# A mixture-of-experts encoder: the overflow part as a small loop ahead of expert 0, and the last tile's norms around the routing

## The chip, the cores and the metric

The kernel runs on one core of a Trainium2 chip. The metric is the device time of one execution in microseconds (us), the median of several runs. The engines have short names: PE is TensorE, which multiplies matrices, with PEld for its weight loads; DVE is VectorE, ACT is ScalarE, POOL is GpSimd, SP is SyncE, which here does little but issue DMA transfers. Each engine works through its own queue of instructions in order and waits on semaphores for the others.

## The reference

Two layers, 512 tokens of 1024 columns. Each layer has a token mixer (two kinds of attention with gates) and a mixture of 16 experts, of which each token uses two; the group of experts and the two inside it are chosen from sigmoid scores. Cut to what the change touches:

```
def _layer_norm(x, g=None, b=None):
    mu = jnp.mean(xf, -1, keepdims=True)
    var = jnp.mean(jnp.square(xf - mu), -1, keepdims=True)
    y = (xf - mu) * lax.rsqrt(var + LN_EPS)
...
def _rms_norm(x, g):
    y = xf * lax.rsqrt(jnp.mean(jnp.square(xf), -1, keepdims=True) + RMS_EPS)
    return (y * g.astype(jnp.float32)).astype(x.dtype)
...
    qa = _apply_rope(_rms_norm(qa.reshape(b, s, A_HEADS, HEAD_DIM), qn_g), cos, sin)
    ka = _apply_rope(_rms_norm(ka.reshape(b, s, A_KV_HEADS, HEAD_DIM), kn_g), cos, sin)
...
def _moe(h, w_router, router_bias, w_gate, w_up, w_down):
    scores = jax.nn.sigmoid((t @ w_router).astype(jnp.float32))
    sel = scores + router_bias.astype(jnp.float32)
    grp_score = jnp.sum(lax.top_k(sel.reshape(-1, N_GROUPS, EXPERTS_PER_GROUP), TOP_K)[0], -1)
    best = jnp.argmax(grp_score, axis=-1)
    ...
    _, idx = lax.top_k(jnp.where(in_group, sel, -jnp.inf), TOP_K)
    ...
    act = jax.nn.silu(hg) * hu * combine[..., None].astype(t.dtype)
    y = jnp.einsum('tef,efd->td', act, w_down)
...
    for l in range(DEPTH):
        ...
        h = _layer_norm(x) * (1.0 + sc1) + sh1
        mix = _mixer(h, w_in[l], q_norm_g[l], k_norm_g[l], w_branch_a[l], w_branch_b[l],
                     w_out[l], cos, sin, slopes)
        x = _layer_norm(DN_ALPHA * x + g1 * mix, ln1_g[l], ln1_b[l])
        h = _layer_norm(x) * (1.0 + sc2) + sh2
        ffn = _moe(h, w_router, router_bias, w_gate, w_up, w_down)
        x = _layer_norm(DN_ALPHA * x + g2 * ffn, ln2_g[l], ln2_b[l])
```

## The kernel before

The 512 tokens are four tiles of 128 (t = 0 to 3). Products are in a split form: an operand is cast to a rounded part (`wH`, `xH`, on ACT) and the rest is subtracted (`wL`, `xL`, on DVE), and PE makes three products of the parts. A scheduler orders the instructions of a stretch of straight code on each engine; a run-time condition (`tc.If`) cuts the program, and nothing is moved across it.

A layer runs through its stages in this order: norm and first modulation, the input projection, rope and attention, the gates, the output projection with the residual, the routing, the experts, and the combine with the last norm.

*Norms.* `stats` makes mean and variance on DVE (`mv`), and `pool_rsqrt` takes the reciprocal root on POOL in two steps, a multiply-add (L285) and a power (L286). `norm` applies it: the first columns by two passes of DVE (L321, L323), the rest, from CUT or CUTH on, by ACT (L319) and two steps of POOL (L325, L326). The rope (`rope(t)`) uses `pool_rsqrt` for the norms of ten heads, the name `rs`: DVE makes the sums of squares `ss`, goes on with products that don't need `rs`, and needs it at L604; `q` follows at L608, and PE transposes it at L620.

*Last tile and routing.* `tile_x1(t)` makes the normed residual x1 and `tile_h2(t)` the second norm h2, which SP stores to `h2d` in memory (L971). After the last tile ACT takes the sigmoid of the scores (L996). DVE and PE make ranks and positions; `vt` (L1066) is the list of tokens of each expert. POOL gathers the rows of h2d for an expert through that list (`xe`, L1104), so the gather needs `vt` and all four stores.

*Experts.* Each expert has room for CAP = 128 tokens. The loop over 16 experts has x_load (the gather, two experts ahead), x_split, x_gate, x_up and x_down; the weights are streamed by SP, 1 MB for each of gate, up and down, with up to ten loads asked for ahead of the routing. `cnti` is the count of the fullest expert. `overflow()` treats what lies over CAP: each engine loads `cnti` (L1204) and branches on it (L1206). It is called in the loop at e == EIF = 5, with NPRE = 4 weight loads issued ahead of it. With these inputs the body isn't entered.

Of the kernel before, what the change touches and what calls it, by code (L numbers as in the profile page):

```python
# [8 lines left out]
F32 = mybir.dt.float32  # L9
# [9 lines left out]
P = 128  # L19
S = 512  # L20
# [67 lines left out]
def build(tc, A, out):  # L88
    nc = tc.nc
    with ExitStack() as es:  # L90
# [192 lines left out]
        def pool_rsqrt(name, src, eps, mult, n):  # L283
            r = small(name, [n])
            PO.tensor_scalar(r, src, mult, eps, op0=OP.mult, op1=OP.add)  # L285
            PO.tensor_tensor(r, r, mhalf[:, :n], op=OP.pow)  # L286
            return r
# [12 lines left out]
        def stats(src):  # L300
# [5 lines left out]
            r = pool_rsqrt("rstd", mv[:, 1:2], LN_EPS, 1.0, 1)  # L306
# [6 lines left out]
        def norm(src, name, g, b, st=None, cut=None):  # L313
# [4 lines left out]
            for p, z in parts(src, cut, D):  # L318
                issued["act"] = ACT.activation(n[:, z], p, AF.Identity, bias=nb, scale=r)  # L319
# [110 lines left out]
        def layer(l, hH, hL, W0, after=None, qk=None):  # L430
# [17 lines left out]
            with ExitStack() as order:  # L448
              if after is not None:
                order.enter_context(tc.issue_after(after.ins))  # L450
              V.tensor_scalar(gq[:, 0, :], gq[:, 0, :], 0.125, None, op0=OP.mult)
# [136 lines left out]
            def rope(t):  # L588
# [5 lines left out]
                rs = pool_rsqrt("rs", ss, RMS_EPS, 1.0 / HD, 10)  # L594
# [344 lines left out]
            x1, r1 = [], []  # L939
# [10 lines left out]
            def tile_x1(t):  # L950
# [9 lines left out]
                n = norm(xr[t], "x1", r_g, r_b, st)  # L960
# [4 lines left out]
            def tile_h2(t):  # L965
# [4 lines left out]
                n2 = norm(n, "h2", r_sc2, r_sh2, st, CUTH)  # L970
                SY.dma_start(h2d[tcols(t), :], n2)  # L971
                if t < NT - 1:
                    ACT.mul(n, n, ALPHA)
# [23 lines left out]
            with tc.issue_after(sig.ins):  # L997
                ACT.mul(x1[NT - 1], x1[NT - 1], ALPHA)
# [17 lines left out]
            two = g4(sel).rearrange("p n (a b) -> p n a b", b=2)  # L1016
            mx, mn = rt("mx", [NTG, 2]), rt("mn", [NTG, 2])
            V.tensor_tensor(mx, two[:, :, :, 0], two[:, :, :, 1], op=OP.max)
            V.tensor_tensor(mn, two[:, :, :, 0], two[:, :, :, 1], op=OP.min)
            gs, gs2 = rt("gs", [NT, NG]), rt("gs2", [NT, NG])  # L1020
            fl = lambda z: z.rearrange("p t g -> p (t g)")
            V.tensor_tensor(fl(gs2), mx[:, :, 0], mx[:, :, 1], op=OP.min)
            V.tensor_tensor(mn[:, :, 0], mn[:, :, 0], mn[:, :, 1], op=OP.max)
            V.tensor_tensor(fl(gs), mx[:, :, 0], mx[:, :, 1], op=OP.max)
            V.tensor_tensor(fl(gs2), fl(gs2), mn[:, :, 0], op=OP.max)
            V.tensor_add(gs, gs, gs2)
# [31 lines left out]
            for k in range(2):  # L1058
                for t in range(NT):
                    at = ats[:, NT * k + t]  # L1060
                    V.tensor_scalar(at, iotab, sv[:, 0, k, t:t + 1], None, op0=OP.is_equal)
                    for i in range(2):
                        PE.matmul(mp, lhsT=at, rhs=src[:, NT * k + t, 2 * i:2 * i + 2], start=(k == 0 and t == 0 and i == 0),
                                  stop=(k == 1 and t == NT - 1 and i == 1))
            vt = small("vt", [2, NE], I32, bufs=1)
# [16 lines left out]
            V.tensor_mul(gm, gm, gt)  # L1082
            go = rt("go", [2, NT])
            V.tensor_sub(go, gt, gm)
            cnt = rt("cnt", [1])
            V.reduce_max(cnt, posf[:, NT, :], axis=X)
            cnti = small("cnti", [1], I32, bufs=1)
            V.tensor_copy(cnti, cnt)

# [97 lines left out]
            def keep_weights():  # L1187

                for i in range(NKEEP):
                    e = NE - NKEEP + i  # L1190
                    we = rt("we", [2, NT])
                    V.tensor_mul(we, o12[:, :, :, e], gm)
                    V.tensor_sub(gm, gm, we)
# [8 lines left out]
            def overflow():  # L1202
# [3 lines left out]
                with tc.If(rv > CAP):  # L1206
                    ovf = sco
                    V.tensor_mul(tmp, o12, go[:, :, :, None].to_broadcast([P, 2, NT, NE]))
                    V.tensor_add(ovf, tmp[:, 0], tmp[:, 1])
                    with tc.For_i(0, NE, 1) as e:  # L1210
                        def blocks(w, tags, view):
                            r = []
                            for i, tag in enumerate(tags):
                                z = wp.tile([P, 512], F32, tag=tag, name="f" + w, bufs=NWH)
                                SY.dma_start(*view(z, A["w_exp_" + w][l][bass.ds(e, 1)], i))
# [8 lines left out]
                        for k in range(2):  # L1224
                            SY.dma_start(fd[k], A["w_exp_down"][l][bass.ds(e, 1)][0, P * k:P * k + P])
                        for t in range(NT):
                            xe = rp.tile([P, D], F32, tag="row", name="fx")
                            SY.dma_start(xe, h2d[tcols(t), :])
                            xT = rp.tile([P, 8, P], F32, tag="row", name="fxT")
# [176 lines left out]
```

## Time and profile before

| | us |
|---|---|
| time before, median of 3 runs (lowest, highest) | 1416.98 (1414.26, 1420.20) |
| profiled execution | 1411.59 |
| its span | 1409.6 |
| PE busy | 1283.9 |
| DVE busy | 1018.3 |
| ACT busy | 717.1 |
| POOL busy | 292.8 |

The span runs from the first to the last instruction that the profiler records; the rest of the execution's time lies around it. Busy times overlap, since the engines run beside each other. The granted clock of PE over the span is 0.954 of full speed. A row of a timeline gives the start, the duration, the engine and the line, then what was written and read; the bracket gives how long the engine was idle before it and which instruction of which engine, or which transfer, released it.

### The profile page before, as it was taken

The page shows a single profiled execution, that of the slowest core. Times are in us where ns is not written, and L with a number is a line of the kernel's source. Part 1 is how long each engine was busy: PE and PEld are TensorE (multiplying, and loading weights), DVE is VectorE, ACT ScalarE, POOL GpSimd, SP SyncE. Part 2 cuts the span into 40 slices and gives each one's busy share as a digit, 9 for nine tenths or more (in the row PEclk, how much of TensorE's full clock was granted, in tenths as well). Part 3 has the DMA queues.
Part 4 walks back from the last instruction along what each step waited for, and adds up shares of the span by engine and source line. Part 5 has one row for each costly group of instructions (what it writes and reads, how often), then busy time and mean ns, then how long its engine had stood idle before and what let it go on. Part 6 is the DMA issues. An engine that isn't in the chain of part 4 may idle for free. (4 is left out here: it accounts for less than half of the span.)

```text
span 1409.6 us, 21666 instructions
## 1 busy us (share of the span) xinstructions
PE 1283.9 (91%) x7953; PEld 1043.7 (74%) x7953; DVE 1018.3 (72%) x1944; ACT 717.1 (51%) x1504; POOL 292.8 (21%) x317
## 2 busy tenths in 40 slices
PE   4898999999998949899889899999999894989986
PEld 4787777677778848788659787767777794878862
DVE  5877877776367779899787876563336767879985
ACT  2344444555744337677554444455564532767760
POOL 1142000000013652222352200000000266122224
PEclk9799999999999969999999999999999996999998
DMA  9646555466066197899644454122215527779952
GB/s 319 213 151 248 197 179 172 150 190 192 30 195 209 60 299 255 275 346 333 240 144 150 150 179 150 61 75 76 75 51 173 196 75 255 263 255 347 355 207 79
DMA packets 182992, 266.77 MB, mean 189 GB/s; under 512 B 18665, under 2 KB 131721, under 8 KB 182880
## 3 DMA queue, kind: packets, MB, share of 16 engines
q1 hardware_dynamic: 159312, 225.46, 48.2%
q0 software_dynamic: 11456, 24.07, 4.9%
q10 hardware_dynamic: 12112, 15.78, 3.7%
q8 instruction: 66, 1.08, 0.3%
q14 instruction: 46, 0.38, 0.1%
HBM read 250.79 MB, written 27.30 MB: 197 GB/s over the span
## 5 line engine op out<-in xcount | busy, mean ns | idle before, releaser
L216 DVE TENSOR_TENSOR wL<-raw,wH 128x512 fp32r<-128x512 f32 x520 | 350.8, 703 | 75.6 <-ACT wH L215 64.3
L215 ACT CAST wH<-raw 128x512 fp32r<-128x512 f32 x520 | 318.3, 622 | 160.2 <-PE mm L1173 41.6
L225 PE MATMUL mm<-hH,wH 128*128 128x512 f32 x512 | 206.9, 404 | 0.0
L226 PE MATMUL mm<-hL,wH 128*128 128x512 f32 x512 | 202.9, 396 | 0.0
L227 PE MATMUL mm<-hH,wL 128*128 128x512 f32 x512 | 202.5, 395 | 0.0
L225 PE MATMUL mm<-wH,xH 128*128 128x256 f32 x512 | 150.5, 294 | 2.0 <-ACT xH L343 1.2
L227 PE MATMUL mm<-wH,xL 128*128 128x256 f32 x512 | 149.4, 292 | 0.7 <-DVE xL L344 0.7
L226 PE MATMUL mm<-wL,xH 128*128 128x256 f32 x512 | 147.4, 288 | 0.7 <-DVE wL L216 0.7
L249 DVE SCALAR_TENSOR_TENSOR acc<-araw,cond,acc 128x512 f32<-128x512 f32 x148 | 110.8, 749 | 5.4 <-DMA araw<-in_w_ada 2.2
L227 PEld LDWEIGHTS mm<-hH,wL 128*128 128x128 f32 x512 | 96.4, 188 | 21.0 <-issue 1.1
L225 PEld LDWEIGHTS mm<-hH,wH 128*128 128x128 f32 x512 | 96.7, 189 | 20.2 <-issue 1.2
L226 PEld LDWEIGHTS mm<-hL,wH 128*128 128x128 f32 x512 | 96.6, 189 | 19.2 <-issue 0.3
L225 PEld LDWEIGHTS mm<-wH,xH 128*128 128x128 f32 x512 | 100.5, 196 | 4.3 <-ACT xH L343 2.1
L226 PEld LDWEIGHTS mm<-wL,xH 128*128 128x128 f32 x512 | 100.0, 195 | 2.6 <-DVE wL L216 1.4
L227 PEld LDWEIGHTS mm<-wH,xL 128*128 128x128 f32 x512 | 99.7, 195 | 1.6 <-DVE xL L344 1.1
L225 PE MATMUL mm<-wH,hH 128*128 128x256 f32 (+1 forms) x272 | 81.5, 300 | 4.8 <-ACT hH L412 3.1
L227 PE MATMUL mm<-wH,hL 128*128 128x256 f32 (+1 forms) x272 | 80.8, 299 | 2.0 <-DVE hL L378 0.7
L226 PE MATMUL mm<-wL,hH 128*128 128x256 f32 (+1 forms) x272 | 80.3, 296 | 0.1
L1178 POOL DMA_INDIRECT y<-ye,vt x28 | 33.5, 1198 | 221.8 <-DVE ye L1174 221.8
L281 POOL DMA_DIRECT2D mod<-adar x8 | 4.2, 531 | 331.1 <-ACT adar L280 331.1
L1173 PE MATMUL mm<-raw,eT 128*128 128x512 f32 x128 | 65.9, 639 | 5.1 <-ACT eT L1156 3.1
L745 DVE TENSOR_TENSOR zB<-sB,biasB 128x256 f32<-128x256 f32 (+2 forms) x48 | 22.9, 488 | 59.9 <-PE sB L743 26.1
(319 smaller groups left out, 2873.9 us busy)
## 6 DMA issues: line engine op xcount, KB each, us to landing
araw<-in_w_ada SPq DMA_DIRECT2D x44, 1024.0 KB, 5.3
raw<-in_w_in SPq DMA_DIRECT2D x40, 1024.0 KB, 5.2
raw<-in_w_exp_gate SPq DMA_DIRECT2D x32, 1024.0 KB, 8.7
raw<-in_w_exp_up SPq DMA_DIRECT2D x28, 1024.0 KB, 9.7
raw<-in_w_exp_down SPq DMA_DIRECT2D x28, 1024.0 KB, 7.5
raw<-in_w_out SPq DMA_DIRECT2D x8, 1024.0 KB, 5.2
y<-y SPq DMA_DIRECT2D x16, 512.0 KB, 8.0
eraw<-in_w_ada SPq DMA_DIRECT2D x4, 1024.0 KB, 14.6
```

The lines of the kernel that those rows point to most:

```text
L215: ACT.copy(H, raw(s))
L216: V.tensor_sub(L, raw(s), H.bitcast(F32))
L225: PE.matmul(o, lhsT=lH, rhs=rH, start=(i == 0), stop=False)
L226: PE.matmul(o, lhsT=lH, rhs=rL, start=False, stop=False)
L227: PE.matmul(o, lhsT=lL, rhs=rH, start=False, stop=(i == n - 1))
L249: last = V.scalar_tensor_tensor(acc, raw[:, k, :], ck, acc, op0=OP.mult, op1=OP.add)
L281: PO.dma_start(moddr[l, kind].rearrange("o (k n) -> (o k) n", n=P), r[0:8, :])
L745: V.tensor_add(z, s[:, :, 0:wid], biasB[g][:, ii::2, j0:j0 + wid])
L1173: PE.matmul(p, lhsT=a, rhs=w, start=(i == 0), stop=(i == len(todo) - 1))
L1178: st = PO.indirect_dma_start(out=y2, out_offset=bass.IndirectOffsetOnAxis(ap=vidx[:, e:e + 1], axis=0), in_=ye, in_offset=None, bounds_che ...
```

## The change

The overflow part is called once ahead of `x_split(0)` and no longer in the loop. Its body loops over the tiles instead of being written out four times, issues its loads on ACT's queue, and stores its rows to `y2` in memory by an indirect DMA, where the combine reads all rows, instead of adding into x1; so the combine uses `gt` for all tokens. `cnti` is reduced straight from the positions. In `pool_rsqrt` the sum with eps is made on DVE and only the power stays on POOL; the factor 1/64 of the head norm goes into eps and the gains. For the last tile, x1 is normed on DVE over all columns; of h2 only the first pass is made ahead of the routing, the second is made of two ACT products and two POOL sums behind the sigmoid, and the store follows them. The group score is the largest of six pair sums instead of two minima and maxima.

```
-        def pool_rsqrt(name, src, eps, mult, n):
+        def pool_rsqrt(name, src, eps, n):
             r = small(name, [n])
-            PO.tensor_scalar(r, src, mult, eps, op0=OP.mult, op1=OP.add)
+            V.tensor_scalar(r, src, eps, None, op0=OP.add)
             PO.tensor_tensor(r, r, mhalf[:, :n], op=OP.pow)
...
-            r = pool_rsqrt("rstd", mv[:, 1:2], LN_EPS, 1.0, 1)
+            r = pool_rsqrt("rstd", mv[:, 1:2], LN_EPS, 1)
...
-            for p, z in parts(src, cut, D):
+            for p, z in parts(src, cut, D) if cut < D else []:
...
-              V.tensor_scalar(gq[:, 0, :], gq[:, 0, :], 0.125, None, op0=OP.mult)
+              V.tensor_scalar(gq[:, 1, :], gq[:, 1, :], 8.0, None, op0=OP.mult)
...
-                rs = pool_rsqrt("rs", ss, RMS_EPS, 1.0 / HD, 10)
+                rs = pool_rsqrt("rs", ss, RMS_EPS * HD, 10)
...
-                n = norm(xr[t], "x1", r_g, r_b, st)
+                n = norm(xr[t], "x1", r_g, r_b, st, D if t == NT - 1 else None)
...
-                n2 = norm(n, "h2", r_sc2, r_sh2, st, CUTH)
+                if t < NT - 1:
+                    n2 = norm(n, "h2", r_sc2, r_sh2, st, CUTH)
+                    ACT.mul(n, n, ALPHA)
+                else:
+                    n2 = f4("h2", [D])
+                    V.scalar_tensor_tensor(n2, n, st[0], r_sc2, op0=OP.subtract, op1=OP.mult)
+                    LAST.append((n2, st[1]))
+                    return
                 SY.dma_start(h2d[tcols(t), :], n2)
-                if t < NT - 1:
-                    ACT.mul(n, n, ALPHA)
...
             sig = ACT.activation(sco, sco, AF.Sigmoid)
             with tc.issue_after(sig.ins):
+                n2, r = LAST[0]
+                for i in range(2):
+                    z = slice(512 * i, 512 * i + 512)
+                    ACT.mul(n2[:, z], n2[:, z], r)
+                    PO.tensor_tensor(n2[:, z], n2[:, z], r_sh2[:, z], op=OP.add)
+                SY.dma_start(h2d[tcols(NT - 1), :], n2)
                 ACT.mul(x1[NT - 1], x1[NT - 1], ALPHA)
...
-            two = g4(sel).rearrange("p n (a b) -> p n a b", b=2)
-            mx, mn = rt("mx", [NTG, 2]), rt("mn", [NTG, 2])
-            V.tensor_tensor(mx, two[:, :, :, 0], two[:, :, :, 1], op=OP.max)
-            V.tensor_tensor(mn, two[:, :, :, 0], two[:, :, :, 1], op=OP.min)
-            gs, gs2 = rt("gs", [NT, NG]), rt("gs2", [NT, NG])
             fl = lambda z: z.rearrange("p t g -> p (t g)")
-            V.tensor_tensor(fl(gs2), mx[:, :, 0], mx[:, :, 1], op=OP.min)
-            V.tensor_tensor(mn[:, :, 0], mn[:, :, 0], mn[:, :, 1], op=OP.max)
-            V.tensor_tensor(fl(gs), mx[:, :, 0], mx[:, :, 1], op=OP.max)
-            V.tensor_tensor(fl(gs2), fl(gs2), mn[:, :, 0], op=OP.max)
-            V.tensor_add(gs, gs, gs2)
+            duo = rt("duo", [NTG, 6])
+            v4s, at = g4(sel), 0
+            for d in range(1, 4):
+                V.tensor_add(duo[:, :, at:at + 4 - d], v4s[:, :, 0:4 - d], v4s[:, :, d:4])
+                at += 4 - d
+            gs = rt("gs", [NT, NG])
+            V.tensor_reduce(fl(gs), duo, axis=X, op=OP.max)
...
+            cnti = small("cnti", [1], I32, bufs=1)
+            V.tensor_reduce(cnti, pos[:, NT, :], axis=X, op=OP.max)
...
-            V.tensor_mul(gm, gm, gt)
-            go = rt("go", [2, NT])
-            V.tensor_sub(go, gt, gm)
-            cnt = rt("cnt", [1])
-            V.reduce_max(cnt, posf[:, NT, :], axis=X)
-            cnti = small("cnti", [1], I32, bufs=1)
-            V.tensor_copy(cnti, cnt)
...
-                    V.tensor_mul(we, o12[:, :, :, e], gm)
-                    V.tensor_sub(gm, gm, we)
+                    V.tensor_mul(we, o12[:, :, :, e], gt)
+                    V.tensor_mul(we, we, gm)
+                    V.tensor_sub(gt, gt, we)
...
                 with tc.If(rv > CAP):
-                    ovf = sco
-                    V.tensor_mul(tmp, o12, go[:, :, :, None].to_broadcast([P, 2, NT, NE]))
-                    V.tensor_add(ovf, tmp[:, 0], tmp[:, 1])
+                    row = rt("row", [2, NT])
+                    V.tensor_scalar(row, sv[:, 0], float(CAP), None, op0=OP.is_ge)
+                    code = rt("code", [2, NT])
+                    encs = enc.rearrange("p (k t) (i j) -> p k t i j", k=2, i=2)
+                    V.tensor_add(code, encs[:, :, :, 0, 0], encs[:, :, :, 1, 0])
+                    V.tensor_mul(row, row, code)
+                    oc = sc("oc", [2, NT, NE])
+                    V.tensor_mul(oc, o12, row[:, :, :, None].to_broadcast([P, 2, NT, NE]))
+                    V.tensor_add(oc[:, 0], oc[:, 0], oc[:, 1])
+                    oi = sc("oi", [NE * NT], I32)
+                    V.tensor_scalar(oi.rearrange("p (e t) -> p t e", t=NT), oc[:, 0], -1.0, float(2 * S), op0=OP.mult, op1=OP.add)
+                    sh = sc("sh", [NE * NT], I32)
                     with tc.For_i(0, NE, 1) as e:
...
-                        for t in range(NT):
-                            xe = rp.tile([P, D], F32, tag="row", name="fx")
-                            SY.dma_start(xe, h2d[tcols(t), :])
-                            xT = rp.tile([P, 8, P], F32, tag="row", name="fxT")
+                            ACT.dma_start(fd[k], A["w_exp_down"][l][bass.ds(e, 1)][0, P * k:P * k + P])
+                        with tc.For_i(0, S, P) as t:
+                            xe = f4("fx", [D])
+                            ACT.dma_start(xe, h2d[bass.ds(t, P), :])
...
+                            PO.indirect_dma_start(
+                                out=y2, out_offset=bass.IndirectOffsetOnAxis(ap=oi[:, 0:1], axis=0),
+                                in_=fy, in_offset=None, bounds_check=2 * S - 1, oob_is_err=False)
...
+            overflow()
             x_split(0)
...
-                if e == EIF:
-                    for ew in [ew for ew in order3[3 * e:] if ew not in PRE][:NPRE]:
-                        PRE[ew] = wraw(x_src(*ew), x_shape(ew[1]), tags[ew])
-                    overflow()
```

On SP, at the end of the loads ahead of the routing in layer 0, before (`h2d` is the second norm in memory, h_4934 that of the last tile, the `raw` names are expert weights):

```order
L192 DMA raw_4963<-in_w_exp_gate 128x8x256
L971 DMA h2d_4265<-h_4934 128x1024
L189 DMA raw_4949<-in_w_exp_up 128x4x256
L189 DMA raw_4950<-in_w_exp_up 128x4x256
L189 DMA raw_4953<-in_w_exp_down 128x1024
L189 DMA raw_4954<-in_w_exp_down 128x1024
L192 DMA raw<-in_w_exp_down 128x2x1024
L192 DMA raw<-in_w_exp_gate 128x8x256
L192 DMA raw<-in_w_exp_up 128x8x256
```

and of the changed kernel:

```order
L192 DMA raw_4955<-in_w_exp_gate 128x8x256
L189 DMA raw_4941<-in_w_exp_up 128x4x256
L189 DMA raw_4942<-in_w_exp_up 128x4x256
L189 DMA raw_4945<-in_w_exp_down 128x1024
L189 DMA raw_4946<-in_w_exp_down 128x1024
L1008 DMA h2d_4265<-h_4931 128x1024
L1207 TENSOR_LOAD cnti
L1209 COMPARE_AND_BRANCH
```

The store of the last tile has moved behind the four loads of the L189 helper, and the branch follows the store.

On PE in layer 0, around the load of the count and its branch, before (`tp` is a transpose, of the token rows `xe` and of the hidden rows `ea` of an expert; `mm` are the products):

```order
L336 MATMUL tp<-c_ident,xe 128x128 x4
L1204 TENSOR_LOAD cnti
L1206 COMPARE_AND_BRANCH
...
L1206 UNCONDITIONAL_BRANCH
L336 MATMUL tp<-c_ident,ea 128x128 x2
L336 MATMUL tp<-c_ident,xe 128x128 x4
L225 MATMUL mm<-wH,xH 128x256
L226 MATMUL mm<-wL,xH 128x256
```

and of the changed kernel:

```order
L1071 MATMUL mp<-src,ats 128x32
L1207 TENSOR_LOAD cnti
L1209 COMPARE_AND_BRANCH
...
L1209 UNCONDITIONAL_BRANCH
L336 MATMUL tp<-c_ident,xe 128x128 x8
L225 MATMUL mm<-wH,xH 128x256
L226 MATMUL mm<-wL,xH 128x256
L227 MATMUL mm<-wH,xL 128x256
```

The branch stood between two transposes of `xe`, and now stands between the last routing product `mp` and the first transpose of `xe` for expert 0.

On DVE in layer 0, from the normalized gates `gt` on, before:

```order
L1079 TENSOR_TENSOR rt_gt<-rt_sv,rt_den 128x8
L216 TENSOR_TENSOR wL<-raw,wH 128x512
L1082 TENSOR_TENSOR rt_gm<-rt_gm,rt_gt 128x8
L216 TENSOR_TENSOR wL<-raw,wH 128x512
L1084 TENSOR_TENSOR rt_go<-rt_gt,rt_gm 128x8
L216 TENSOR_TENSOR wL<-raw,wH 128x512
L1192 TENSOR_TENSOR rt_we<-rt_o_5001,rt_gm 128x8
L1193 TENSOR_TENSOR rt_gm<-rt_gm,rt_we 128x8
L1194 TENSOR_TENSOR rt_we<-rt_we 128x4
L344 TENSOR_TENSOR xL<-tp,xH 128x512 x2
L216 TENSOR_TENSOR wL<-raw,wH 128x512 x4
L1136 TENSOR_TENSOR ea<-ea,mm 128x256
```

and of the changed kernel:

```order
L1196 TENSOR_TENSOR rt_gt<-rt_gt,rt_we 128x8
L1197 TENSOR_TENSOR rt_we<-rt_we 128x4
L1207 TENSOR_LOAD cnti
L1209 COMPARE_AND_BRANCH
L1211 TENSOR_SCALAR rt_row<-rt_sv 128x8
...
L1209 UNCONDITIONAL_BRANCH
L216 TENSOR_TENSOR wL<-raw,wH 128x512 x3
L344 TENSOR_TENSOR xL<-tp,xH 128x512
L216 TENSOR_TENSOR wL<-raw,wH 128x512
L344 TENSOR_TENSOR xL<-tp,xH 128x512
L216 TENSOR_TENSOR wL<-raw,wH 128x512 x6
```

The subtractions `wL` that stood between the small routing steps now stand behind the branch, three of them ahead of the first `xL`.

## Rows read from the trace of the kernel before

**Rows 1.** The page, part 1: engine, busy us (share of the span), instructions.

```profile
PE 1283.9 (91%) x7953; PEld 1043.7 (74%) x7953; DVE 1018.3 (72%) x1944; ACT 717.1 (51%) x1504; POOL 292.8 (21%) x317
```

**Rows 2.** Times by stretch: us; busy per engine (count); clock, DMA share, GB/s.

```profile
560.38:570.62 10.24, 10.16 (x69) 8.69 (x68) 8.41 (x15) 6.04 (x12) 2.52 (x2) 1.00 0.97 315
570.62:585.93 15.31, 11.82 (x71) 10.20 (x70) 11.10 (x18) 9.76 (x19) 2.22 (x2) 0.89 0.62 203
585.93:596.30 10.37, 10.29 (x70) 8.81 (x69) 9.54 (x18) 8.01 (x16) 2.52 (x2) 1.00 1.02 339
...
1246.91:1263.66 16.75, 12.50 (x71) 10.45 (x70) 11.09 (x18) 9.76 (x19) 2.22 (x2) 0.90 0.55 176
```

**Rows 3.** Lines L1206, L1204 (ns min/median/max) and the matmul behind, from the timeline.

```profile
L1206 PEldq COMPARE_BRANCH  x2: 3836/3968/4101, 569.4 to 1245.5; - x2
...
L1206 DVEq COMPARE_BRANCH  x2: 56/64/72, 572.6 to 1248.6; - x2
...
L1204 PEldq TENSOR_LOAD <-cnti x2: 314/402/490, 568.8 to 1245.1; - x2
...
573.78 0.66 PE L336 MATMUL tp<-c_ident,ea 128*128 128x128 f32 x2 [2.75 <-PEq L1206]
```

**Rows 4.** Timeline ahead of expert 0: start us, us, work [idle <-releaser].

```profile
515.78 1.94 PE L336 MATMUL tp<-c_ident,xe 128*128 128x128 f32 x8 [5.87 <-DMA xe<-h2d,vt]
...
1192.41 1.94 PE L336 MATMUL tp<-c_ident,xe 128*128 128x128 f32 x8 [5.95 <-DMA xe<-h2d,vt]
...
510.98 1.44 POOL L1104 DMA_INDIRECT xe<-h2d,vt  x1 [4.19 <-DVE rt_cnt L1086]
```

**Rows 5.** Timeline of DVE in expert 0.

```profile
520.18 0.69 DVE L216 TENSOR_TENSOR wL<-raw,wH 128x512 fp32r<-128x512 f32 x1 [1.11 <-ACT wH L215]
```

**Rows 6.** Timeline from the last tile's norm to the list of tokens.

```profile
499.33 0.69 DVE L303 BATCH_NORM_STATS2 st<-x 128x6 f32<-128x512 f32 x1 [1.66 <-POOL x L326]
...
502.37 0.49 ACT L319 ACTIVATE h<-x,nb,rstd 128x128 f32<-128x128 f32 x1 [4.68 <-POOL nb L308]
...
509.95 0.19 DVE L1066 TENSOR_TENSOR vt<-c_none,mp 128x32 int32<-128x32 f32 x1 [0.25 <-PE mp L1063]
```

**Rows 7.** Timeline of SP's issues: start us, us to issue.

```profile
493.84 0.49 SPq L192 DMA_DIRECT2D raw<-in_w_exp_gate  x1
504.15 0.34 SPq L971 DMA_DIRECT2D h2d<-h  x1
```

**Rows 8.** DMA issued at 493.84, 504.15, 555.49, 556.01, 1169.58: KB, us to landing.

```profile
raw<-in_w_exp_gate SPq DMA_DIRECT2D x1, 1024.0 KB, 10.3
...
h2d<-h SPq DMA_DIRECT2D x1, 512.0 KB, 3.1
...
raw<-in_w_exp_gate SPq DMA_DIRECT2D x1, 1024.0 KB, 7.4
...
raw<-in_w_exp_up SPq DMA_DIRECT2D x1, 1024.0 KB, 12.6
...
raw<-in_w_exp_gate SPq DMA_DIRECT2D x1, 1024.0 KB, 9.8
```

**Rows 9.** Lines L285, L286; PE's waits in 75:130 and 720:806 (us, times, longest).

```profile
L285 POOL TENSOR_SCALAR rs<-ss x8: 308/3020/3658, 80.3 to 791.1; 128x10 f32<-128x10 f32 x8
...
L286 POOL TENSOR_TENSOR rs<-rs,c_mhalf x8: 1954/1962/3074, 81.8 to 792.6; 128x10 f32<-128x10 f32 x8
...
PE tp L620 <- DVE q L608: 4.0, 3, 2.2
...
PE tp L620 <- DVE q L608: 4.9, 2, 2.7
```

**Rows 10.** Timeline of POOL in the tail.

```profile
1397.75 0.18 POOL L285 TENSOR_SCALAR rstd<-mv 128x1 f32<-128x1 f32 x1 [0.96 <-DVE mv L305]
```

**Rows 11.** DMA issued at 581.04 and 643.18: KB, us to landing.

```profile
raw<-in_w_exp_gate SPq DMA_DIRECT2D x1, 1024.0 KB, 5.7
...
raw<-in_w_exp_gate SPq DMA_DIRECT2D x1, 1024.0 KB, 12.7
```

## What the change was predicted to do

> **What bounds the kernel now.** I read the page first: TensorE (PE) is busy for 91% of the span [rows 1]. So a microsecond is to be had only where PE stands still or runs at a lower granted clock, and for each edit I asked what ended PE's idle time there. Next came the table of engine times by stretch of the expert loop: an expert takes 10.2 to 10.4 us with PE busy for all but 0.1 of it, but the stretch in which expert 5 begins, where the skip of the overflow part stands, takes 15.31 us in layer 0 and 16.75 in layer 1, with PE busy for 11.82 and 12.50 and a mean clock of 0.89 and 0.90 instead of 1.00 [rows 2]. The timeline and the branch's own line tell why [rows 3]: PE's compare-and-branch lasts 3.8 to 4.1 us, DVE's under 0.1, and the matmul behind it names it as the releaser. After that the timeline just ahead of expert 0: PE has nothing to do for 5.87 and 5.95 us there, until the gathered tokens `xe` land [rows 4]. Last come the places of the smaller edits.
>
> **The change, part by part.** All terms are set against the profiled execution, 1411.59 us of which 1409.6 are its span. It lies 5.4 below the median of 1416.98, so I add the sum of the terms to the median.
>
> *The overflow test.* Its body never runs in this trace, so only the skip counts: a register load of `cnti` on each engine, a branch on each, and what the cut through the program costs. In its old place that is 15.31 - 10.35 = 5.0 us in layer 0 and 16.75 - 10.35 = 6.4 us in layer 1, with 10.35 for an ordinary expert, close to the neighbour behind [rows 2]: **-11.4 us**, if nothing of it comes back. In the new place PE's load (0.5) and its branch (4.1 at most) follow the last small matmul of the routing, at 509.9, and end at 514.5. The `xe` that PE waits for lands at 515.78 [rows 3, 4], so 1.3 us of cover are left, and I cost the branch at nothing. Without the cover it would cost up to 4.6 per layer. The clock has nothing to lose there, since PE has stood idle.
>
> The other engines lose work that they had done in that wait. VectorE (DVE) subtracted six weight pieces (`wL`) ahead of expert 0; in the new order three of them stand behind the branch and ahead of `xL`, three after. ScalarE (ACT) gains three weight casts and a table load between the branch and `xH`. A subtraction takes 0.69 us, so three are 2.1 us, but DVE sat waiting for `wH` ahead of four of them in this stretch, 1.11 us ahead of the first [rows 5], which is where they fit. Bounds 0 to +2.1 per layer; I take +0.3, nearer to nothing by that row: **+0.6**.
>
> GpSimd (POOL) and SP each hold the branch too. Behind it on POOL stand the gathers of experts 2 to 4, on SP the later weight loads; they would be late by the wait for `cnti` and 1 us, and nobody asks for them within that.
>
> *The last tile's norms.* Before, x1's last 256 columns go over ACT and POOL, and DVE waits 1.66 us for POOL ahead of the second statistics. After, DVE makes all 1024 columns in its two passes (about 0.3 us longer each), which gains some 1.1. The sigmoid no longer stands behind ACT's piece of h2 (0.5), which makes about 1.6; fewer operations for the group score give another 0.2 or so. So `vt`, the list of tokens that the gather reads, comes some 1.8 us earlier than 509.95 [rows 6].
>
> But the gather also needs h2 in memory, and its last store is moved in the queue. Before, SP issues it at 504.15 and four half-megabyte weight loads behind it [rows 7]; it lands in 3.1 us, at 507.3, and `vt` is the later one. In the new order those four loads stand ahead of the store, and I find nothing that they must wait for, so they go out right behind the gate load of 493.84. The store needs the sigmoid (about 501.1), two ACT products and a POOL sum behind them, and is issued at about 504.9. Transfers from one queue land in the order of issue: a gate load took 7.4 us, and an up load issued 0.5 later took 12.6 [rows 8]. The gate load of 493.84 lands at 504.1 (10.3 later); the four loads are 2.1 MB, at the 339 GB/s of rows 2 another 6.2 us, to 510.3; the store's half megabyte takes 1.5 to 2.7 more, to 511.8 to 513.0. So the gather starts at about 512.4 where it started at 510.98: +1.4, less 0.3 for less traffic beside it. The gather is the one that PE waits for [rows 4]. In layer 1 the gate load ahead lands 0.5 sooner after its issue (9.8, not 10.3 [rows 8]), and I take nothing there. **+1.1** in all, bounds -5 (the store is not held up) and +3.
>
> *The rope's reciprocal root.* POOL's small multiply-add (128x10) becomes a DVE addition. On POOL it needs 0.3 us at the least, but 3.0 as the median of eight and up to 3.66, beside a DVE that works back to back; the power of 1.95 follows it [rows 9]. DVE then waits for the power, and PE for DVE's q: 4.0 us in three waits in layer 0 and 4.9 in two in layer 1. All of these gone would be -8.9. At the least it is nothing: the power itself reads the same memory, and could be held just as long. But the longest of eight powers took 3.07, so even a held one is over sooner than a held multiply-add and a power after it; I take 0.6 for each of five waits, **-3.0**, nearer to nothing. The Trainium skill, "SBUF — State Buffer", section "Who interferes with whom", says that DVE's second pair of ports is shared with GpSimd under an exclusive lock. The 3.66 us for 10 columns agree with it; by that rule the power would be held in the multiply-add's stead, which is the third rival below.
>
> *The other norms.* In each tile's norm POOL's first step (0.18 in the tail, with a hand-over) becomes a DVE step of about 0.15 behind DVE's own; the tail and the change of layer each have four tiles in a row on that chain [rows 10]: 8 x 0.1 = **-0.8**, bounds 0 and -1.5. The smaller combine (`gt` used as it stands) lies on idle DVE: nothing.
>
> Sum: -11.4 + 0.6 + 1.1 - 3.0 - 0.8 = **-13.5**; 1416.98 - 13.5 = 1403.5, **1403 us**.
>
> **The rivals.**
> 1. *The store is not held behind the loads* (they wait for something, or the queue doesn't hold it). Then `vt` decides: heads -4 instead of +1, about **1398**. Against it: rows 8. Chance 0.12.
> 2. *The rope waits go altogether*, -8.9 and some half-clock time behind them instead of -3: **1396**. For it: PE's waits there hang on the power alone. Chance 0.13.
> 3. *POOL's power is held as long as the multiply-add was*: rope 0, **1406**. Chance 0.17.
> 4. *The skip costs as much in its new place* (the change doesn't do what it says): if it takes some 6 us on PE instead of 4.6, or `xe` comes earlier by 4, or the cut keeps ACT and DVE from their preparations, up to 5 per layer come back: **1413**, no change. For it: cover of only 1.3 us. Against it: PE's branch was the longest, and it starts when PE is idle. Chance 0.09.
> 5. *The weight stream becomes the bound* (slower). Gate loads issued at 581.04 and 643.18 took 5.7 and 12.7 us [rows 11]: behind the pause of the old place the backlog of transfers grows by 7.0 us in six experts, some 1.1 each, at 339 GB/s. The pause was what let it drain; without it about 5 us more are outstanding. An expert would then take 10.35 + 1.1 once the lead is used up. With n experts of each layer so bound it costs 2 x 1.1 x n: the gain is gone at n = 6, and at n = 10 the time is **1425**. It decides from the point where the lead, of which the trace shows only that it bears 12.7 us, is used up before the middle of the loop. Against it: PE waits for no transfer in the loop, busy 10.29 of 10.37. Chance 0.05 for slower; a loss of a few us by it is in the range.
>
> The forecast itself has 0.44. The Trainium skill, "Runtime: NRT & Kernel Launch", section "Instruction fetch mechanics", says that a taken branch to a far target must fetch its instructions first, an ifetch stall. PE's 3.8 to 4.1 us against 0.06 on DVE [rows 3] agree; by it a shorter body is not cheaper as long as its end is far, and in the new place the fetch lies in PE's wait, which gives the same sum.
>
> **How the numbers follow.** Rivals 1 and 2 together would give 1391, rivals 3 and 4 together 1416. With the bounds of the casts (+4.2) and of the stream's first losses, and the measured spread of some 3 us, 8 in 10 lie between 1393 and 1411. A measurement of this kernel can tell 0.5%, 7 us, from no change: faster means below 1409.9. The forecast and rivals 1 to 3 (0.86) lie there, of which 0.02 for added small losses goes to no change; rival 4 and this are no change, 0.11; slower 0.05; faster 0.84.
>
> **What would show it.** In the profile after: the stretch of expert 5 at 10.4 us like its neighbours; PE's branch ahead of expert 0 with the matmul on `xe` still released by the transfer, not by the branch; the last store's landing after `vt`, and PE's first expert beginning 1 us later after the last tile's norm than now, not 2 us earlier; POOL's power in the rope at 1.95 or stretched to over 3; PE's waits for q between 0 and 9 us. The prediction is wrong if PE is released by the branch in the new place, if matmuls in the loop wait for `raw`, or if the gather runs ahead of the landing that I computed.

## The result and the profile after

The changed kernel takes 1398.68 us (median of 4 runs, 1394.19 to 1399.36) against 1415.67 for the kernel before on the same chip; the ratio is 0.9873, 95% interval 0.9849 to 0.9896. The forecast was 1403 us, 1393 to 1411. The profiled execution went from 1411.59 to 1398.57 us, which is -13.0 where the sum of the terms said -13.5. But the sum came out for partly wrong reasons: two terms missed by what they left out, one explanation was wrong, and the largest term holds in full only for an execution like the one it was read from.

The same marked instructions in both traces show where the time went (start in us; the difference is the after less the before, and its step to the next mark is what the stretch between gained or lost):

| mark | before | after | difference |
|---|---|---|---|
| a product ahead of the rope, layer 0 | 88.78 | 89.00 | +0.2 |
| a product behind it | 184.06 | 183.82 | -0.2 |
| last router product, layer 0 | 495.92 | 494.95 | -1.0 |
| first `xe` on PE | 515.78 | 517.16 | +1.4 |
| `ea` of expert 0 | 525.63 | 526.85 | +1.2 |
| `ea` of expert 14 | 679.13 | 675.43 | -3.7 |
| `ea` of expert 15 | 693.44 | 691.09 | -2.4 |
| a product ahead of the rope, layer 1 | 757.32 | 754.66 | -2.7 |
| a product behind it | 885.90 | 880.21 | -5.7 |
| last router product, layer 1 | 1171.58 | 1165.18 | -6.4 |
| first `xe` on PE | 1192.41 | 1185.58 | -6.8 |
| `ea` of expert 0 | 1201.90 | 1195.53 | -6.4 |
| `ea` of expert 15 | 1371.22 | 1358.56 | -12.7 |
| end of the span | 1409.6 | 1396.8 | -12.8 |

The page after, its first lines (those of before are [rows 1]):

```profile
span 1396.8 us, 21644 instructions
...
PE 1278.9 (92%) x7953; PEld 1039.7 (74%) x7953; DVE 1024.2 (73%) x1974; ACT 720.2 (52%) x1506; POOL 282.4 (20%) x273
```

The times by stretch where expert 5 begins, to be read beside [rows 2] (the columns are the same; the last row is layer 1):

```profile
561.58:571.93 10.35, 10.27 (x70) 8.79 (x69) 9.52 (x18) 8.01 (x16) 2.53 (x2) 1.00 0.99 312
571.93:582.29 10.36, 10.28 (x70) 8.81 (x69) 9.53 (x18) 8.02 (x16) 2.54 (x2) 1.00 0.84 275
...
1240.58:1250.95 10.37, 10.29 (x70) 8.81 (x69) 9.53 (x17) 8.00 (x16) 2.54 (x2) 1.00 0.81 264
```

The stretches of 15.31 and 16.75 us are now like their neighbours. PE's branch and the first matmul on `xe` in the new place, from the branch's line and the timeline (beside [rows 3, 4]):

```profile
L1209 PEldq COMPARE_BRANCH  x2: 236/295/354, 510.3 to 1180.1; - x2
...
517.16 1.94 PE L336 MATMUL tp<-c_ident,xe 128*128 128x128 f32 x8 [7.18 <-DMA xe<-h2d,vt]
...
1185.58 1.94 PE L336 MATMUL tp<-c_ident,xe 128*128 128x128 f32 x8 [5.69 <-DMA xe<-h2d,vt]
```

PE is still released by the transfer, and the branch lasts 0.24 to 0.35 us, not 3.8 to 4.1. The wait ahead of expert 0 in layer 0 has grown from 5.87 to 7.18 us. The timeline between the sigmoid and the gather there shows why:

```profile
501.70 2.49 POOL L1007 TENSOR_TENSOR h<-h,row 128x512 f32<-128x512 f32 x2 [0.85 <-ACT h L1006]
...
501.92 1.15 DVE L1022 TENSOR_TENSOR versus<-rt_sel 128x48 f32<-128x48 f32 x1
502.96 1.27 DVE L1021 TENSOR_TENSOR versus<-rt_gs 128x12 f32<-128x12 f32 x1
504.14 0.17 DVE L1022 TENSOR_TENSOR versus<-rt_gs 128x12 f32<-128x12 f32 x1
...
504.13 2.73 POOL L1100 MEMSET xe<- 128x1024 f32 x3
...
505.88 1.03 DVE L1041 TENSOR_SCALAR asgb<-rt_rank 128x64 bf16<-128x64 f32 x1
...
510.02 0.19 DVE L1076 TENSOR_TENSOR vt<-c_none,mp 128x32 int32<-128x32 f32 x1 [0.25 <-PE mp L1071]
...
512.59 1.19 POOL L1106 DMA_INDIRECT xe<-h2d,vt  x1 [5.73 <-DVE rt_we L1197]
```

While POOL makes its two new sums (501.70 to 504.19), two tiny VectorE steps take 1.15 and 1.27 us, and the same step of 128x12 a moment later 0.17. Then POOL's zeroing of `xe` runs to 506.86, and `asgb`, 64 columns, takes 1.03 and ends only with it. So `vt` comes at 510.02, where it came at 509.95 [rows 6], though the routing's first step (`rt_sel`) had begun 2.2 us sooner, at 501.04 instead of 503.20. And the gather follows `vt` by 2.57 us, not by 1.03. That it waits for the store is not shown by this trace, which lacks the landing; the runs below show it.

### The profile page after: what moved, and what is told of

Its sections match the earlier page's. It is cut to its first block, busy times and chain, and to the rows that moved or that the text cites. A ratio compares the mean times of both kernels' runs of the same rounds, so it can differ in the third digit from the quotient of the medians.

```text
span 1396.8 us, 21644 instructions
## 1 busy us (share of the span) xinstructions
PE 1278.9 (92%) x7953; PEld 1039.7 (74%) x7953; DVE 1024.2 (73%) x1974; ACT 720.2 (52%) x1506; POOL 282.4 (20%) x273
```

## The experiments

Each run is compared with the kernel before on the same chip. Distances "from the router" are counted from the start of the last router product of the layer.

### Is it the place of the test, or the size of its body?

Back in the old place, with the new, small body; its scratch moves to other tiles (not shown):

```
...
-            overflow()
             x_split(0)
...
+                if e == EIF:
+                    for ew in [ew for ew in order3[3 * e:] if ew not in PRE][:NPRE]:
+                        PRE[ew] = wraw(x_src(*ew), x_shape(ew[1]), tags[ew])
+                    overflow()
...
```

> The changed kernel with its small overflow loop back in the old place, ahead of expert 5 (its scratch lies in other tiles, the rest is as changed). Theory PLACE: the 4 us of PE's branch and the 5.0 and 6.4 us that expert 5 lost come from a branch in the midst of PE's work; then PE's branch lasts about 4 us here too, expert 5 takes 15.3 and 16.7 us, and the time is about 1398.7 + 11 = 1410 us. Theory SIZE: PE's branch is long when the body that it jumps over is long (four tiles written out, some 240 matrix instructions with their weight loads, against some 60 in the loop); then the branch lasts about 0.3 us, expert 5 takes 11.5 to 12.5 us (the load of the count and the engines' drain remain), and the time is 1400 to 1403 us.

Ratio 0.9956 (0.9930 to 0.9982), 1407.81 us. The branch's line, the times by stretch over expert 5 (layers 0 and 1), and PE behind the branch:

```profile
L1209 PEldq COMPARE_BRANCH  x2: 323/338/353, 569.5 to 1241.7; - x2
...
570.70:586.30 15.60, 12.37 (x71) 10.32 (x69) 11.00 (x18) 9.65 (x18) 2.22 (x2) 0.89 0.58 201
...
1243.20:1256.70 13.50, 10.54 (x71) 8.90 (x70) 10.89 (x19) 9.80 (x19) 2.22 (x2) 1.00 0.67 222
...
573.32 0.41 PE L336 MATMUL tp<-c_ident,ea 128*128 128x128 f32 x2 [2.17 <-DVEq L1209]
```

Each theory was half right. The branch is short with the small body, as SIZE said; the expert still loses 5.2 and 3.1 us, near to what PLACE said for layer 0. PE now waits for VectorE's branch instead of its own, 2.17 us instead of 2.75 [rows 3]: each engine loads the count and branches, and PE starts again when VectorE is through. In layer 0 the mean clock of the stretch is 0.89, as in the kernel before; in layer 1 it stayed at 1.00, and there the loss is 2.1 us smaller.

The run root_only (its edit comes further down) has the test as before, large body and old place, so it is a second execution of the old test. Its branch and the two stretches of expert 5:

```profile
L1206 PEldq COMPARE_BRANCH  x2: 3761/4168/4576, 573.3 to 1245.6; - x2
...
574.57:588.74 14.17, 10.75 (x71) 8.93 (x70) 10.93 (x18) 9.77 (x19) 2.22 (x2) 1.00 0.66 203
1247.07:1261.88 14.81, 10.75 (x71) 8.93 (x70) 10.93 (x18) 9.76 (x19) 2.23 (x2) 1.00 0.62 195
```

There the clock stayed at 1.00 in both layers, and the old test lost 3.8 and 4.5 us, 8.3 in all and not 11.4. So at the full clock a test in the midst of PE's work costs 3.1 us with the small body and 3.8 to 4.5 with the large one: most is the stop itself, the length of the branch adds about 1. Where the clock fell for a part of the stretch behind the pause, 1.1 to 2.1 us come on top, and whether it falls differs between executions and layers.

The opposite: the new place, with the four tiles of the body written out (the scratch tiles change too, not shown).

```
...
-                        with tc.For_i(0, S, P) as t:
-                            xe = f4("fx", [D])
-                            ACT.dma_start(xe, h2d[bass.ds(t, P), :])
+                        for t in range(0, S, P):
+                            ACT.dma_start(xe, h2d[t:t + P, :])
...
```

> The changed kernel with the loop over the four tiles in the overflow body written out again, in its new place ahead of expert 0. PLACE: PE's branch lasts 0.3 us as in the changed kernel. SIZE: it lasts about 4 us, from 510.3 to 514.3 in layer 0, and still ends ahead of the landing of xe that PE waits for (517.2 us in layer 0, in layer 1 with 1 us to spare), so the time is 1399 us by both, within 2.

Ratio 0.9887 (0.9839 to 0.9935), 1399.22 us, as forecast. small_at_5 ran beside it on the same chip, so the place is worth 8.6 us there, with the small body in the old one.

```profile
L1209 PEldq COMPARE_BRANCH  x2: 1985/2764/3542, 511.1 to 1180.3; - x2
```

The body's size takes the branch from 0.3 to 2.0 and 3.5 us, and in the new place that costs nothing that the runs can tell. The Trainium skill, "Runtime: NRT & Kernel Launch", section "Instruction fetch mechanics", says that a taken branch stalls for a fetch when its target lies outside the instructions already held. The branch over some 60 PE instructions (30 matmuls with their weight loads) and the one over some 240 agree with it. That PE fetched in these microseconds is not shown: the traces have no instruction transfers by engine.

What the test costs in its new place is priced by leaving the overflow part out (the call of `overflow()` is gone):

> The changed kernel without the overflow part: neither the load of the count, nor the test, nor the body (left out: the tokens over an expert's capacity, of which these inputs have none). It prices the test in its new place. Theory: nothing, PE waits for xe there anyway: 1397 to 1399 us, and the first ea at the same distance from the landing of xe. Rival: the casts and subtractions that could not be made ahead cost up to 2 us per layer: 1395 us.

Ratio 0.9897 (0.9848 to 0.9947), 1401.76 us: not faster than with the test, as far as these runs tell. In layer 0 the first `xe` comes 7.1 us behind the start of the gather, where it is 4.6 in the changed kernel. The timeline of POOL, DVE and PE in no_overflow:

```profile
515.38 2.93 POOL L1106 DMA_INDIRECT xe<-h2d,vt  x1 [5.84 <-DVE wL L216]
...
515.35 1.89 DVE L216 TENSOR_TENSOR wL<-raw,wH 128x512 fp32r<-128x512 f32 x3
...
522.49 0.88 PE L336 MATMUL tp<-c_ident,xe 128*128 128x128 f32 x3 [9.84 <-DMA xe<-h2d,vt]
```

Without a test VectorE goes straight on to the weight pieces, and the issue of the gather on POOL takes 2.93 us beside three of them in a row, instead of 1.19. In small_at_5 (layer 0) it took 2.76 in the same company. In the changed kernel the three subtractions stand behind the test and begin 0.38 us after the gather, which then loses nothing. So the test costs nothing there, and in layer 0 it spared 1.7 us. That is one layer of one execution: in layer 1 of the same run the gather took 1.27 without a test, and where the store came later still (layer 0 of changed_again and zero_on_act) it fell among the subtractions behind the test and took 1.54 and 1.66.

The first `ea` was expected at the same distance from `xe`, and came nearer: 8.8 us instead of 9.7 in layer 0. That is the clock, not the casts. PE is busy the whole way in both, at a mean clock of 0.71 with the test and 0.78 without:

```profile
517.16:526.85 9.69, 9.69 (x58) 9.20 (x59) 5.77 (x9) 7.42 (x13) 2.18 (x3) 0.71 0.97 347
...
522.49:531.30 8.81, 8.81 (x58) 8.58 (x59) 4.08 (x6) 5.86 (x10) 1.62 (x2) 0.78 0.89 297
```

### What the last tile's rearrangement does

Undone, with all else as changed:

```
-                n = norm(xr[t], "x1", r_g, r_b, st, D if t == NT - 1 else None)
+                n = norm(xr[t], "x1", r_g, r_b, st)
...
+                n2 = norm(n, "h2", r_sc2, r_sh2, st, CUTH)
+                SY.dma_start(h2d[tcols(t), :], n2)
```

> The changed kernel with the last tile's norms and its store as before (the rest, the group score too, as changed). Theory: the rearrangement gains nothing in all, because in layer 0 the store lands late behind four weight loads and in both layers POOL's zeroing of xe ends at the same time and holds DVE's routing; so vt and the gather come within 0.5 us of the changed kernel in layer 1 and the gather 1.5 us earlier in layer 0: 1396 to 1399 us. Rival: the norms are worth their 1.6 us per layer and would be missed: 1402 us.

Ratio 0.9881 (0.9833 to 0.9930), 1399.18 us, the same as with it as far as these runs tell. From the router `vt` comes at 15.16 and 14.60 us (changed: 15.07 and 14.75) and the first `xe` at 20.74 and 20.43 (changed: 22.21 and 20.40). The sigmoid does come later (8.17 and 7.43 instead of 5.80 and 5.47), so the 2 us are there, and are lost before `vt`: here the step of 128x12 takes 0.18 us and `asgb` 0.29.

Three runs then mend the suspects one at a time. First the store ahead of the four weight loads:

```
             for e, w, tag in AHEADW[:HOLD]:
-                PRE[e, w] = wraw(x_src(e, w), x_shape(w), tag)
+                if tag != "f4":
+                    PRE[e, w] = wraw(x_src(e, w), x_shape(w), tag)
...
+            with tc.issue_after(stored.ins):
+                for e, w, tag in AHEADW[:HOLD]:
+                    if tag == "f4":
+                        PRE[e, w] = wraw(x_src(e, w), x_shape(w), tag)
```

> The changed kernel with the four half-megabyte weight loads issued behind the last tile's store of h2 instead of ahead of it. Theory: in layer 0 the store lands 3.1 us after its issue instead of 7.5, and the first gather is released by the list of tokens again, 1.0 us behind it, instead of 2.6: the first xe is 1.6 us earlier counted from the last tile's router matmul (20.6 instead of 22.2), in layer 1 as now; time 1396 to 1398 us. Rival: the store was not held up by the loads, and nothing moves.

The first `xe` in layer 0 stands at 20.29 us from the router instead of 22.21, and the gather follows `vt` by 1.08 instead of 2.57; the other 0.4 us are an earlier `vt` in this execution. The time, 1399.69 us (0.9901, 0.9862 to 0.9940), doesn't show it: the 4 runs spread over 11.6 us. That the store was held is also plain where the trace has its landing, as in unrolled_ahead (DMA issued at 504.98, then the gather):

```profile
h2d<-h SPq DMA_DIRECT2D x1, 512.0 KB, 7.5
...
513.33 1.19 POOL L1106 DMA_INDIRECT xe<-h2d,vt  x1 [5.71 <-DVE rt_we L1197]
```

7.5 us to landing where the kernel before has 3.1 [rows 8], and the gather 0.9 behind it.

Second, the zeroing of `xe` on ScalarE:

```
-                PO.memset(z, 0.0)
+                    ACT.mul(z, r_sh2, 0.0)
```

> The changed kernel with the zeroing of the three xe tiles on ScalarE instead of GpSimd. Theory: GpSimd's zeroing ends 11.9 us after the last router matmul and holds VectorE's two-fold copies of the ranks (asgb and rt_o, 1.03 and 0.99 us instead of 0.29), so without it vt comes 0.7 to 0.8 us earlier in both layers; the gather gains that in layer 1 (15.0 instead of 15.8) and nothing in layer 0, where the store's landing releases it; time 1397 to 1398 us. Rival: those two are slow for another reason, vt stays at 15.06.

```profile
506.05 0.20 DVE L1041 TENSOR_SCALAR asgb<-rt_rank 128x64 bf16<-128x64 f32 x1
```

`asgb` takes 0.20 instead of 1.03, and `vt` comes 0.76 and 0.81 us earlier, as expected. The gather gained only 0.12 in layer 1 (15.64, expected 15.0): it now follows `vt` by 1.7 us, by more than the 1.0 of a free gather, so something else is last. This trace has no landing of that store; it was issued at 8.90 us from the router, and in layer 1 of unrolled_ahead and small_at_5 it took 6.0 and 5.9 us, which would be 14.9 here, an estimate that makes the store the last again. In layer 0, where nothing was expected, the gather came 1.2 us later than in the changed kernel (18.87 from the router) and the first `xe` at 24.01; changed_again has 18.80 there, 0.9 behind a landing that took 8.6 us. 1398.37 us (0.9890, 0.9857 to 0.9923).

Third, with the store first, the last tile's second pass of h2 as one VectorE instruction in place of two ACT products and two POOL sums:

```
-                for i in range(2):
-                    z = slice(512 * i, 512 * i + 512)
-                    ACT.mul(n2[:, z], n2[:, z], r)
-                    PO.tensor_tensor(n2[:, z], n2[:, z], r_sh2[:, z], op=OP.add)
+                V.scalar_tensor_tensor(n2, n2, r, r_sh2, op0=OP.mult, op1=OP.add)
```

> As store_first, and the last tile's second pass of h2 is one VectorE instruction (128x1024, times the reciprocal root plus the shift, about 1.28 us, 0.3 of it in the wait for the sigmoid) instead of two ScalarE products and two GpSimd sums. Theory: the GpSimd sums held VectorE's small routing steps (1.15 and 1.27 us instead of 0.2), so VectorE loses 1.0 us to the new step but gains 2.1, and GpSimd's zeroing ends 3 us earlier and holds nobody (another 1.4): vt at 13.0 to 13.7 instead of 15.06, the gather at 14 to 14.7 in both layers instead of 17.6 and 15.8, and the time 4 to 5 us below the changed kernel: 1394 us, better than both kernels. Rival: VectorE's own step costs what it frees, vt at 15 and the time as store_first.

```profile
500.29 1.28 DVE L1005 SCALAR_TENSOR_TENSOR h<-h,rstd,row 128x1024 f32<-128x1024 f32 x1
...
502.47 0.18 DVE L1023 TENSOR_TENSOR versus<-rt_gs 128x12 f32<-128x12 f32 x1
...
504.30 0.20 DVE L1043 TENSOR_SCALAR asgb<-rt_rank 128x64 bf16<-128x64 f32 x1
...
513.29 1.94 PE L336 MATMUL tp<-c_ident,xe 128*128 128x128 f32 x8 [5.65 <-DMA xe<-h2d,vt]
```

The step of 128x12 takes 0.18 again and `asgb` 0.20. From the router `vt` comes at 13.07 and 12.61 us and the first `xe` at 18.68 and 18.23, where store_first has 20.29 and 20.62. 1394.45 us; ratio 0.9848 (0.9818 to 0.9879). Beside the changed kernel on one chip:

> The changed kernel as it is, beside the next run on the same chip, so that the two can be compared: ratio to the kernel before 0.987 to 0.990.

> The kernel of the run sum_on_dve once more, beside the changed kernel on the same chip. Theory: 4 us below the changed kernel, as the distances from the last router matmul to the first xe have shown (22.2 to 18.7 and 20.4 to 18.2 us): ratio to the kernel before 0.984 to 0.987. Rival: the 4 us are lost again in the expert loop, where the weights then come too late, and the two are the same.

The changed kernel took 1399.70 us (0.9903, 0.9883 to 0.9923), a little outside what was expected, and the version with the sum on VectorE 1395.41 (0.9870, 0.9844 to 0.9896). It is 4.3 us lower in the median. The intervals of the ratios overlap, but all six runs of it (1388.23 to 1397.54) lie below all six of the changed kernel (1397.86 to 1405.21), and the distances from the router show where it comes from: the first `xe` at 23.65 and 22.27 us in the changed kernel, at 19.30 and 18.34 here. The loop takes nothing back; an expert takes 10.34 to 10.37 us from expert 3 on, save the last. In this profile of the changed kernel the store was held in layer 1 as well (issued 9.27 and landed 16.77 us from the router, the gather at 17.62), so in layer 1 it depends on the execution.

### The reciprocal root by itself

The kernel before, with only the change in `pool_rsqrt` and its factors (the factors not shown):

```
...
-            PO.tensor_scalar(r, src, mult, eps, op0=OP.mult, op1=OP.add)
+            V.tensor_scalar(r, src, eps, None, op0=OP.add)
...
```

> The kernel before, with one part of the change: the sum with eps of the reciprocal root goes from GpSimd to VectorE. Theory HELD: in the rope the power is held as long as VectorE runs back to back, and ends 1.9 us after VectorE's last instruction; each of VectorE's waits for it falls by 0.3 us (2.15 to 1.85), the two layers gain 0.5 to 3 us with the clock, and the time is 0 to 4 us below the kernel before. Theory FREE: the power runs beside VectorE, the waits go, and the time is 9 to 12 us below.

Ratio 0.9963 (0.9948 to 0.9978), 1408.43 us, 4.4 less: just past HELD's end. In its trace the two ropes take 1.8 and 3.0 us less than before. VectorE's waits for the power in the two ropes (us, times, longest), the same in this run and in the changed kernel:

```profile
DVE ra L604 <- POOL rs L286: 5.2, 3, 1.9
...
DVE ra L604 <- POOL rs L286: 3.7, 2, 1.9
```

They were 13.1 us in seven waits before. The changed kernel's timeline of one tile shows the power held:

```profile
89.86 4.75 POOL L286 TENSOR_TENSOR rs<-rs,c_mhalf 128x10 f32<-128x10 f32 x1 [6.14 <-DVE rs L285]
...
92.09 0.69 DVE L216 TENSOR_TENSOR wL<-raw,wH 128x512 fp32r<-128x512 f32 x1
...
94.64 0.83 DVE L604 TENSOR_TENSOR ra<-ra,rs 128x640 f32<-128x640 f32 x1 [1.86 <-POOL rs L286]
```

It starts at once and ends at 94.61, 1.83 us behind VectorE's last instruction: alone it needs 1.95 [rows 9], so it gets next to nothing done beside VectorE. A wait of 2.15 becomes 1.86. The rule of "SBUF — State Buffer", section "Who interferes with whom", in the Trainium skill (an exclusive lock on the shared ports) agrees with these rows, and with the VectorE step of 1.27 us beside POOL's sums.

## Why the prediction was right, and where not

**The overflow test (-11.4).** Right in size for the two profiled executions: from the first `ea` to the last but one in layer 0 it is -4.9 us, and in layer 1's loop -6.3, together -11.2. But that is in part luck. The 11.4 was read from one execution, in which the clock fell in both layers; in root_only the same test cost 8.3, and the place alone is worth 8.6 in the times. Right that its new place is covered by the wait for `xe`, and that the clock has nothing to lose there: it stood at 0.50, the lower of its two levels (1.2 GHz), from 510.00 to 517.10. Wrong in the cause: I took PE's branch of 4 us for what made expert 5 late. With a branch of 0.34 us the old place still cost 5.2 and 3.1. And "a shorter body is not cheaper as long as its end is far" missed what the change does: the body of one tile is short enough for a short branch. That saves only about 1 us in the old place, since the other engines are nearly as late.

**The casts (+0.6).** From the first `xe` to the first `ea` it is -0.2 in layer 0 and +0.5 in layer 1, +0.3 in all. PE is busy for the whole of these stretches before and after, so no cast or subtraction holds it, and the idle time took them in, as [rows 5] had it. What differs is the mean clock: 0.68 before and 0.71 after in layer 0, 0.71 and 0.69 in layer 1.

**The last tile and the heads (+1.1).** From the router to the first `xe` it is +2.35 in layer 0 and -0.43 in layer 1, +1.9. The failed step is "`vt` comes some 1.8 us earlier": `vt` came 1.0 us later and 0.2 earlier, counted from the router. The 1.0 is partly the execution's: with the old norms `vt` came at 14.03 and 14.92 us in the trace of before, at 14.60 to 15.16 in root_only and old_norms, and with the new ones at 14.68 to 15.07 in the changed kernel and the runs that leave its norms and its zeroing as they are. None of them has the 1.8. I had put POOL's two sums on the store's path alone and not asked what they, and the zeroing behind them, do to VectorE's routing beside them, though I had weighed the very same conflict in the rope. The store's part was right in kind: issued at 504.22, gather at 512.59, where I said 504.9 and 512.4. Counted from the router, though, the gather came at 17.64 us, where the forecast's 512.4 is 16.5, and in changed_again the store was held in layer 1 too, where I took nothing.

**The rope (-3.0).** -0.5 in layer 0 and -3.0 in layer 1. The sum fits; the mechanism is that of the third rival, though its price of nothing was wrong. The power is held in the multiply-add's stead, and each of VectorE's waits lost about 0.3 us or, where the wait was short, went altogether. That a held power "is over sooner than a held multiply-add and a power after it" was right, but the 0.6 us for each wait was too much: in one tile the pair took 5.37 us before (90.45 to 95.82), the addition and the held power take 5.01 after (89.60 to 94.61). PE's waits for q fell by only 1.2 us, 8.9 to 7.7. The rest in layer 1 is half-clock time. The stretch of its rope, before and after (PE's busy time stands behind the length, the mean clock third from the end):

```profile
757.32:885.90 128.58, 123.64 (x765) 102.62 (x763) 97.28 (x199) 55.43 (x130) 19.09 (x10) 0.97 0.47 154
...
754.66:880.21 125.55, 122.26 (x765) 101.30 (x764) 97.59 (x203) 55.51 (x130) 16.13 (x6) 0.99 0.48 158
```

PE stands still for 3.3 us instead of 4.9, and does the same 765 matmuls in 1.4 us less, with the clock at 0.99 instead of 0.97: 3.0 together. Before, the clock was low from 800 to 806 (0.55), behind a wait of 2.7 us; PE's longest wait there is now 1.9 us. root_only repeats the stretch, 125.55 us, so it is the reciprocal root that does it; that the shorter wait is what spares the clock is argued, not shown.

**The other norms (-0.8).** Change of layer and tail gave -0.3 and -0.1. But I forgot the output stage, where the same step stands in the path to the router: -1.4 and -0.8 up to the last router product, counted from the last product of the gates (`gate`, L915). How much of that is the norms and not chance was not tried by itself; root_only, with the same norms in that stage, shows 0.8 more in layer 0 and 0.7 less in layer 1. The stretch took 64.0 and 63.9 us before and 61.9 to 64.9 in the traces of all other runs, so this gain is not told from chance.

**What no term held.** The last expert of layer 0 took 15.66 us instead of 14.31. Over the other traces it took 14.25 to 15.93 in layer 0, in the same code, so it is the execution's; its cause stays open. The transfers' backlog, of the fifth rival, did not grow by 5 us: the gate load issued at 649.84 took 13.1 us against 12.7 at 643.18 [rows 11].

## What to carry to other kernels

A run-time test costs what it takes to stop and restart all engines at its place; put it where the busiest engine waits anyway, and its branch, long or short, is free as long as it ends before the wait does. Read the price of such a stop from more than one execution, since the clock may fall behind it or not. When work is moved to an idle GpSimd, look at what VectorE does beside it: a step that costs GpSimd nothing can stretch a chain of tiny VectorE steps by more than it saved. And look at where a store stands in its queue: it belongs ahead of the loads that nobody is waiting for.

## What was not expected of the hardware

How long PE's branch takes follows the length of what it skips: 0.24 to 0.35 us over some 60 PE instructions, 2.0 to 3.5 over some 240, 3.8 to 4.6 with the body of the kernel before. The issue of the first indirect gather on GpSimd took 1.18 to 1.19 us where VectorE made only small routing steps or began its subtractions 0.38 us or more after it, and 2.76 and 2.93 where it began with three of them in a row. And a test can help: leaving it out made the first gather of layer 0 slower, when VectorE no longer stood still.
